# A fused diffusion-layer kernel whose instruction order comes from a planner in the kernel file: 46 shifts of places in the planner's list, and a bound on the row loads of the late modulation

## The chip, the cores and the metric

One core of one Trainium2 chip. The metric is the device time of one execution in microseconds (us); for the kernel before it is the median of 3 runs. TensorE (PE in the profile) multiplies matrices, VectorE (DVE) and ScalarE (ACT) work on rows of 128 partitions, GpSimd (POOL) clears some memory and issues a few DMAs, SyncE (SP) issues all other DMAs. Each engine takes its own instructions in the order in which they stand in the program, and waits at the first one whose operands aren't there.

## The reference

One layer for 512 latent tokens x and 256 context tokens, model width 1024, all in float32:

```python
mod = silu(c) @ w_ada + b_ada                  # six vectors of 1024: sh1 sc1 gt1 sh2 sc2 gt2
h  = rms_norm(x, g_norm1)*(1 + sc1) + sh1      # and hc from the context likewise
aq, ak, av, dq, dk, dv, dz, da, db, ga, gd = split_cols(h @ w_in)
y_attn = window_ctx_attention(q_a, k_a, v_a, k_ac, v_ac, attn_sink)
o_dl   = bidir_delta(*dn_inputs(dq, dk, dv, da, db), s_cf, s_cb)   # gated delta rule, chunks of 64
y = sigmoid(ga)*(y_attn @ w_br_attn) + sigmoid(gd)*(y_d @ w_br_dn)
x_new = x + gt1 * (y @ w_out)
x_new = x_new + gt2 * (square(relu(hm @ w_mlp1)) @ w_mlp2)         # hm: normed x_new with sc2, sh2
```

The delta rule runs forward and backward over 4 context chunks and then 8 latent chunks; each chunk needs the inverse of a triangular matrix. The late modulation is the last four of the six vectors of `mod` (gt1, sh2, sc2, gt2): they aren't needed before the output product.

## The kernel before, in words

Weights and activations are split into a high and a low part, and a product is three matmuls: high by high, high by low, low by high (`mm3`, L308, its matmuls at L313 to L315; the gate tiles at L1060; `prod`, L1547, in the feed-forward part, where Strassen-like combinations of blocks are used). `wload` (L283) loads a weight tile of 128 x 1024 on SyncE's queue (L286), ScalarE casts the high part (L291), VectorE subtracts for the low part (L296). `act` (L182) is the helper of all table functions on ScalarE, `split` (L221, L222) that of high and low parts.

The stages overlap, and in order they are: the first modulation and the norms (L246 to L321); the input products; attention (`scores` L550, `outputs` L609; L565 to L655); the chunk matrices and their inversion (L806 to L895, the inverse is a row-by-row recurrence on VectorE at L884 and L885); `combine` (L897), which joins halves of the inverses by 32x32 matmuls (L905, L906, L915, L916); the recurrence `chain_step` (L1159, matmuls of 64x64 at L1176); the gate tiles and attention's branch products that fill in between (L1060, L1106); the output products; the feed-forward part.

The late modulation (`late_mod`, L1120) has 32 rows, 8 for each of the four vectors. A row is a tile of 128 x 1024 of `w_ada` (512 KB): one DMA on SyncE's queue (L1124), one multiply with the silu of c and a sum on VectorE (L1125), one column of `modT`. The rows' tiles come from the common arena of memory, so a load waits only until its place in the arena is free. The rows are asked for in three places: three and three ahead of the two `combine` of the latent chunks and the two masked products behind them (L1306, L1318), one at a time inside the recurrence (L1356), the rest at the output products (L1436, L1439) and in the feed-forward part.

The code writes 8,024 steps (instructions) in the order of its lines: 5,857 for TensorE, 1,074 for VectorE, 849 for ScalarE, 38 for GpSimd, 206 for SyncE. `arrange` (L1804) then gives each engine its final order. `needs` (L1749) lists which steps a step must follow. `listed` (L1817) is a list planner: it walks forward in planned time with a cost for each step (`Step.cost`, L1727); on each engine it takes, of the steps that are ready by plan, the one that stands earliest in the code. On TensorE it prefers a step with the same kind of tile (whole 128x128 or smaller) if that one stands at most 50 places later. It also plans the DMA queues and the fetching of TensorE's program in blocks of 256 instructions. `gangs` are the groups of small matmuls of the recurrence, which become ready together. The planned times are used for nothing else: on the chip each engine takes its list in order, and real waits decide the times.

Of the kernel before, what the change touches and what calls it, by code (L numbers as in the profile page):

```python
# [14 lines left out]
ALU = mybir.AluOpType  # L15
# [19 lines left out]
NPL = ()  # L35
WEARLY = 0
STICK = 50
LIMIT = 1e9
ND1 = 3
NGD = 5  # L40
P = 128
# [34 lines left out]
class Buf:  # L76


    def __init__(self, arena, start, n, ap):
        self.arena, self.start, self.n, self.ap = arena, start, n, ap  # L80
# [36 lines left out]
def tile_layer(ctx: ExitStack, tc: tile.TileContext, I: dict, out: bass.AP, dbg=None):  # L117
    nc = tc.nc
    V, A, G, PE = nc.vector, nc.scalar, nc.gpsimd, nc.tensor
# [47 lines left out]
    ties, gangs = [], []  # L167
    nosync = mybir.DependencyInfo(mybir.DependencyClass.NoSync, mybir.DependencyReason.DATA)

    def tie(later, name):  # L170
        tc.add_manual_dep(later, name, nosync, reason="order")
        ties.append((later.name, name))

    def act(out_, in_, func, **kw):
# [942 lines left out]

    modT = const.tile([P, 4, 8], F32, name="modT")

    def late_mod(grp):  # L1120

        for j in range(8):
            wa = alloc(1024)
            nc.sync.dma_start(out=wa.ap, in_=I["wada2"][grp, j])  # L1124
            V.scalar_tensor_tensor(wa.ap, wa.ap, 0.5, scr.ap, op0=ALU.mult, op1=ALU.mult, accum_out=modT[:, grp, j:j + 1])  # L1125
            wa.free()
            if j == 7:
                V.tensor_tensor(modT[:, grp], modT[:, grp], bada[:, 16 + 8 * grp:24 + 8 * grp], op=ALU.add)
            yield
# [619 lines left out]
def needs(steps, ties):  # L1749

    at = {s.name: k for k, s in enumerate(steps)}
    before = [set() for _ in steps]
    for later, name in ties:
        before[at[later]].add(at[name])
    users, rings = {}, {tag: [] for tag in Step.RINGS}
    for k, s in enumerate(steps):
        for t in s.tiles:
            tag = t.split("_")[0]
            if tag in rings:
                if t not in users:  # L1760
                    rings[tag].append(t)
                users.setdefault(t, []).append(k)
    for tag, ts in rings.items():
        for old, new in zip(ts, ts[Step.RINGS[tag]:]):
            before[users[new][0]].update(users[old])
        for old, new in zip(ts, ts[1:]):
            before[users[new][0]].add(users[old][0])
    places = {}
    for k, s in enumerate(steps):
        for t, place in s.tiles.items():  # L1770
            if place:
                places.setdefault(t, (place, []))[1].append(k)
    for n, (place, ks) in enumerate(list(places.values())):
        gate = len(before)
        before.append(set())
        for (lo, hi), old in list(places.values())[:n]:
            if lo < place[1] and place[0] < hi:
                before[gate].update(k for k in old if k < ks[0])
                for o in (o for o in old if o > ks[0]):
                    before[o].update(k for k in ks if k < o)  # L1780
                    for k in (k for k in ks if k > o):
                        before[k].add(o)
        for k in ks:
            before[k].add(gate)
    wrote, read = {}, {}
    for k, s in enumerate(steps):
        for c in s.reads:
            if c in wrote:
                before[k].add(wrote[c])
        for c in s.writes:  # L1790
            before[k].update(read.pop(c, ()))
            if c in wrote:
                before[k].add(wrote[c])
            wrote[c] = k
        for c in s.reads:
            read.setdefault(c, []).append(k)
        before[k].discard(k)
    return before
# [5 lines left out]
def arrange(tc, nc, ties, gangs):  # L1804

    steps = [Step(i) for i in nc.cur_bb.bb.instructions if "Boundary" not in type(i).__name__]
    before = needs(steps, ties)
    order = mybir.DependencyInfo(mybir.DependencyClass.NoSync, mybir.DependencyReason.DATA)
    last = {}
    for k in listed(steps, before, gangs):  # L1810
        s = steps[k]
        if s.eng in last:
            tc.add_manual_dep(s.ins, last[s.eng], order, reason="order")
        last[s.eng] = s.name


def listed(steps, before, gangs):  # L1817

    n = len(steps)
    at = {s.name: k for k, s in enumerate(steps)}  # L1820
    gang = {at[name]: g for g in gangs for name in g}
    wait = {id(g): len(g) for g in gangs}
    after, left, ready = [[] for _ in before], [len(b) for b in before], [0.] * len(before)
    for k, b in enumerate(before):
        for p in b:
            if k in gang and gang[k] is gang.get(p):
                left[k] -= 1
            else:
                after[p].append(k)
    engines = ("PE", "DVE", "Activation", "Pool", "SP")  # L1830
    free, links = dict.fromkeys(engines, 0.), {"SP": 3200., "Pool": 0.}
    free["SP"] = 750.
    coming, here, out = {e: [] for e in engines}, {e: [] for e in engines}, []
    flight, whole, cold = [], True, False
    words, asked = 0, {n: 0. for n in range(3)}

    def release(ks, at_):
        for k in ks:
            ready[k] = max(ready[k], at_(k))
            left[k] -= 1  # L1840
            if not left[k]:
                if k in gang:
                    g = gang[k]
                    wait[id(g)] -= 1
                    if not wait[id(g)]:
                        go = max(ready[at[x]] for x in g)
                        for x in g:
                            heapq.heappush(coming["PE"], (go, at[x]))
                elif k < n:
                    heapq.heappush(coming[steps[k].eng], (ready[k], k))  # L1850
                else:
                    release(after[k], lambda _: ready[k])

    first = [k for k, m in enumerate(left) if not m]
    for k in first:
        left[k] = 1
    release(first, lambda _: 0.)
    for _ in steps:
        t, e = min((free[e] if here[e] else max(free[e], coming[e][0][0]), e) for e in engines if here[e] or coming[e])
        while coming[e] and coming[e][0][0] <= t:  # L1860
            heapq.heappush(here[e], heapq.heappop(coming[e])[1])
        k = here[e][0]
        if e == "PE":
            same = min((x for x in here[e] if steps[x].whole == whole), default=k)
            if same <= k + STICK:
                k = same
            block = int(words / 256 - .54) + 1
            if not steps[k].whole and asked.get(block, 0) - t > LIMIT * ((block + .54) * 256 - words):
                k = min((x for x in here[e] if steps[x].whole and steps[x].dtype.endswith("32r")), default=k)
        here[e].remove(k)  # L1870
        heapq.heapify(here[e])
        s = steps[k]
        out.append(k)
        if s.dma and e == "SP":
            if len(flight) >= 8:
                t = max(t, flight[-8])
            links[e] = end = max(t + (2400 if s.bytes > 100000 else 1600), links[e]) + s.bytes / 422
            flight.append(end)
            own = 400
        elif s.dma:  # L1880
            links[e] = end = max(t + 2400, links[e]) + s.bytes / 159
            own = 900
        else:
            own, lag = s.cost()
            if e == "PE":
                one = s.dtype.endswith("32r") or s.dtype.endswith("16") or s.ins.is_transpose
                words, had = words + (2 if one else 4), words
                block = int(words / 256 + .63)
                if block > int(had / 256 + .63):
                    asked[block] = max(t + 1100, links["SP"] - 500) + 1250  # L1890
                t = max(t, asked.get(int(had / 256 - .54), 0))
                if s.whole != whole:
                    t += 92 if whole else 130
                    cold = whole = s.whole
                elif cold and whole and s.dtype.endswith("32r"):
                    t, cold = t + 100, False
            end = t + lag
        free[e] = t + own

        def seen(x):  # L1900
            if x >= n:
                return end + 40
            f = steps[x].eng
            if not s.dma and f == e:
                return free[e] if e == "PE" else end + 10
            return end + SEEN[f]

        release(after[k], seen)
    return out


def _constants():
# [108 lines left out]
```

## Time and profile before

| | us |
|---|---|
| median of 3 runs | 898.63 (896.56 to 899.63) |
| the profiled execution | 897.89 |
| its span, first to last instruction | 896.1 |
| TensorE busy | 863.9 |
| VectorE busy | 652.8 |
| ScalarE busy | 495.3 |
| mean granted TensorE clock | 0.994 |

The span is the time from the first to the last instruction of the program; the execution's own time has some 1.8 us more around it. "Busy" is the union of an engine's instruction times. Matmuls are pipelined, so a busy TensorE needn't be at its peak. In the rows of the profile, L is a line of the kernel, the arrow in "out<-in" points from an instruction's inputs to its output, and the "<-" behind an idle time names what ended it. A row that merges several instructions gives their count behind an x.

### The profile page before, as it was taken

To read this page: it belongs to the slowest core of one execution; us is meant where nothing else is said; L and a number is where in the kernel's file an instruction comes from. 1 tells how busy PE (TensorE), PEld (TensorE's weight loads), DVE (VectorE), ACT (ScalarE), POOL (GpSimd) and SP (SyncE) were. 2 spreads that over 40 slices of the span, in tenths; PEclk is the share of its full clock that TensorE was granted. 3 is DMA by queue.
4 is the path that set the end of the run, shared out by engine and by line. 5 is a ranking of instruction groups with operands and counts; after the bars stand their busy time and mean duration, and the time that the engine had idled before them with its cause. 6 is when DMAs were issued, how large, how long until landed. Compare 5 with 4: busy or idle time off the path is not lost.

```text
span 896.1 us, 18017 instructions
## 1 busy us (share of the span) xinstructions
PE 863.9 (96%) x7564; PEld 719.5 (80%) x7564; DVE 652.8 (73%) x1111; ACT 495.3 (55%) x881; POOL 26.1 (3%) x42
## 2 busy tenths in 40 slices
PE   8999999999998998899999999999999999999998
PEld 6777778877776776777777799888997899889886
DVE  5756899977768998757787778893868377638631
ACT  5559774486668795577754335561554255425520
POOL 0000010010000001100000000000000000000000
PEclk9999999999999998999999999999999999999999
DMA  9824455442111227523144653634314331333031
GB/s 353 327 98 95 95 140 114 101 89 54 36 36 35 62 94 277 196 73 98 50 153 166 205 182 118 209 121 128 108 48 136 100 131 58 116 111 103 1 117 47
DMA packets 31985, 107.13 MB, mean 120 GB/s; under 512 B 4000, under 2 KB 4512, under 8 KB 31904
## 3 DMA queue, kind: packets, MB, share of 16 engines
q1 hardware_dynamic: 29600, 97.59, 32.2%
q0 software_dynamic: 2304, 8.39, 5.8%
q8 instruction: 59, 0.97, 0.4%
q14 instruction: 22, 0.18, 0.1%
HBM read 103.87 MB, written 2.10 MB: 118 GB/s over the span
## 4 chain that ended last, share of the span: by engine, by line
PE 65%; DVE 16%; ACT 11%; DMA 5%; issue 3%; SPq 1%; ACTq 0%; DVEq 0%
PE banks L1060 12%; PE banks L1547 11%; PE banks L314 11%; PE banks L315 11%; PE banks L313 11%; ACT m L182 3%; PE banks L1176 3%; DVE m L222 2%; DVE m L885 2%; DVE m L884 1%; ACT m L221 1%; DMA m<-in_wada 1%; DMA m<-in_wm 1%; DVE st L589 1%; ACT wh L291 1%
## 5 line engine op out<-in xcount | busy, mean ns | idle before, releaser
L313 PE MATMUL banks<-m,wh 128*128 128x512 f32 (+1 forms) x568 | 213.6, 376 | 1.4 <-ACT wh L291 1.4
L314 PE MATMUL banks<-m,wh 128*128 128x512 f32 (+1 forms) x568 | 210.4, 370 | 1.1 <-DVE m L222 1.1
L315 PE MATMUL banks<-m,wl 128*128 128x512 f32 (+1 forms) x568 | 210.5, 371 | 0.8 <-DVE wl L296 0.8
L291 ACT ACTIVATE wh<-wr 128x1024 fp32r<-128x1024 f32 (+1 forms) x92 | 90.4, 984 | 128.3 <-PE banks L314 92.3
L221 ACT ACTIVATE m<-m 128x512 fp32r<-128x512 f32 (+2 forms) x118 | 81.9, 720 | 82.4 <-PE banks L1547 18.9
L1547 PE MATMUL banks<-m,m 128*128 128x256 f32 x1008 | 123.3, 284 | 3.6 <-ACT m L221 3.1
L1547 PEld LDWEIGHTS banks<-m,m 128*128 128x128 f32 x1008 | 122.0, 192 | 5.1 <-ACT m L221 3.7
L313 PEld LDWEIGHTS banks<-m,wh 128*128 128x128 f32 x568 | 107.1, 189 | 20.7 <-ACT wh L291 2.2
L315 PEld LDWEIGHTS banks<-m,wl 128*128 128x128 f32 x568 | 106.9, 188 | 20.9 <-DVE wl L296 2.1
L314 PEld LDWEIGHTS banks<-m,wh 128*128 128x128 f32 x568 | 107.1, 189 | 18.8 <-DVE m L222 1.4
L1060 PE MATMUL banks<-m,wh 128*128 128x512 f32 x320 | 106.8, 410 | 3.6 <-ACT m L182 3.1
L222 DVE TENSOR_TENSOR m<-m,m 128x512 fp32r<-128x512 f32 (+2 forms) x118 | 92.4, 805 | 22.6 <-ACT m L221 15.8
L296 DVE TENSOR_TENSOR wl<-wr,wh 128x1024 fp32r<-128x1024 f32 (+1 forms) x76 | 84.3, 1110 | 22.9 <-ACT wh L291 17.7
L1674 DVE SCALAR_TENSOR_TENSOR m<-banks,modT,m 128x512 f32<-128x512 f32 x32 | 24.0, 750 | 74.2 <-PE banks L315 74.1
L1060 PEld LDWEIGHTS banks<-m,wh 128*128 128x128 f32 x320 | 60.1, 193 | 16.7 <-ACT m L182 3.4
L1060 PE MATMUL banks<-m,wl 128*128 128x512 f32 x160 | 65.3, 409 | 0.9 <-DVE wl L296 0.9
L314 PE MATMUL banks<-m,m 128*128 128x256 f32 (+1 forms) x136 | 45.7, 342 | 0.5 <-DVE m L321 0.5
L313 PE MATMUL banks<-m,m 128*128 128x256 f32 (+1 forms) x136 | 45.0, 345 | 0.9 <-ACT m L320 0.8
L315 PE MATMUL banks<-m,m 128*128 128x256 f32 (+1 forms) x136 | 44.5, 336 | 0.2 <-DVE m L296 0.2
L1125 DVE SCALAR_TENSOR_TENSOR m<-m,m 128x1024 f32<-128x1024 f32 x32 | 38.7, 1220 | 6.6 <-DMA m<-in_wada 6.6
L1176 PEld LDWEIGHTS banks<-m,m 64*64 64x64 f32 x1600 | 26.8, 134 | 13.6 <-issue 3.8
L1060 PEld LDWEIGHTS banks<-m,wl 128*128 128x128 f32 x160 | 30.8, 192 | 8.1 <-DVE wl L296 1.3
(252 smaller groups left out, 1318.2 us busy)
## 6 DMA issues: line engine op xcount, KB each, us to landing
m<-in_wada SPq DMA_DIRECT2D x48, 512.0 KB, 5.4
wr<-in_wm SPq DMA_DIRECT2D x40, 512.0 KB, 3.6
wr<-in_win SPq DMA_DIRECT2D x39, 512.0 KB, 3.6
m<-in_wm SPq DMA_DIRECT2D x24, 512.0 KB, 3.7
wl<-in_win POOLq DMA_DIRECT2D x16, 512.0 KB, 5.6
m<-in_xT SPq DMA_DIRECT2D x8, 512.0 KB, 5.7
wr<-in_wbr SPq DMA_DIRECT2D x16, 256.0 KB, 2.6
wr<-in_wout SPq DMA_DIRECT2D x8, 512.0 KB, 3.9
```

Source lines behind the costliest of these rows:

```text
L182: r = A.activation(out_, in_, func, **kw)
L221: A.activation(r32(hi), src, AF.Copy)
L222: (eng or V).tensor_tensor(r32(lo), src, hi, op=ALU.subtract)
L291: upper[0] = A.activation(r32(hi), raw, AF.Copy)
L296: V.tensor_tensor(r32(lo), raw, hi, op=ALU.subtract)
L313: PE.matmul(acc, w[0][:, k, :], xhi, start=(start and i == 0), stop=False)
L314: PE.matmul(acc, w[0][:, k, :], xlo, start=False, stop=False)
L315: r = PE.matmul(acc, w[1][:, k, :], xhi, start=False, stop=(stop and i == n - 1))
L1060: PE.matmul(acc.ap, w[x][:, k, :], hx[k][y], start=(k == p == 0), stop=(k == KT - 1 and p == 2))
L1125: V.scalar_tensor_tensor(wa.ap, wa.ap, 0.5, scr.ap, op0=ALU.mult, op1=ALU.mult, accum_out=modT[:, grp, j:j + 1])
L1176: runs[n].append(PE.matmul(out_, w, x, start=True, stop=True).ins.name)
L1547: PE.matmul(dst, r32(self.w[w][i][:, k * P:(k + 1) * P]), xs7[x][k][j], start=(n == 0), stop=(n == 11))
```

## The change

Three things. First, row n of the late modulation may be loaded only after the sum of row n - 3: a real wait in the DMA's own queue, and also a constraint for the planner. Second, the planner is rewritten as a class `Lists` whose `run` takes a `rank` for every step in place of the step's number, and ready steps are taken by the smallest rank. The members of a gang carry the rank of the gang's first member. Third, `settled` starts from rank = number and adds 46 shifts. An entry (engine, first, end, places) adds `places` to the rank of the steps first to end - 1 of one engine (0 TensorE, 1 VectorE, 2 ScalarE; -1 means all engines). A positive shift lets other ready steps go first, a negative one lets these go first. No instruction is added, removed or changed. The constant `LIMIT` and the branch that used it go.

```diff
-LIMIT = 1e9
+NROWS = 3
...
-    def tie(later, name):
-        tc.add_manual_dep(later, name, nosync, reason="order")
+    sync = mybir.DependencyInfo(mybir.DependencyClass.Sync, mybir.DependencyReason.DATA)
+
+    def tie(later, name, how=nosync):
+        tc.add_manual_dep(later, name, how, reason="order")
         ties.append((later.name, name))
...
+    sums = []
+
     def late_mod(grp):
 
         for j in range(8):
             wa = alloc(1024)
-            nc.sync.dma_start(out=wa.ap, in_=I["wada2"][grp, j])
-            V.scalar_tensor_tensor(wa.ap, wa.ap, 0.5, scr.ap, op0=ALU.mult, op1=ALU.mult, accum_out=modT[:, grp, j:j + 1])
+            d = nc.sync.dma_start(out=wa.ap, in_=I["wada2"][grp, j])
+            if len(sums) >= NROWS:
+                tie(d.ins, sums[-NROWS], sync)
+            r = V.scalar_tensor_tensor(wa.ap, wa.ap, 0.5, scr.ap, op0=ALU.mult, op1=ALU.mult, accum_out=modT[:, grp, j:j + 1])
+            sums.append(r.ins.name)
             wa.free()
...
-    before = needs(steps, ties)
...
-    for k in listed(steps, before, gangs):
+    for k in settled(Lists(steps, needs(steps, ties), gangs)):
...
-            block = int(words / 256 - .54) + 1
-            if not steps[k].whole and asked.get(block, 0) - t > LIMIT * ((block + .54) * 256 - words):
-                k = min((x for x in here[e] if steps[x].whole and steps[x].dtype.endswith("32r")), default=k)
...
+SHIFTS = (
+    (2, 1816, 2816, 200), (2, 535, 735, 250), (1, 5382, 5442, -40), (-1, 6758, 6788, -160), (0, 176, 196, -80),
+    (0, 341, 1841, 5), (1, 3561, 3636, 250), (2, 1435, 2435, 200), (1, 5696, 6296, 80), (-1, 6202, 7202, -80),
+    (0, 4946, 5146, -15), (-1, 345, 1345, -30), (-1, 1367, 1427, 30), (0, 15, 1015, 80), (-1, 1714, 1814, 20),
+    (-1, 6311, 7311, 40), (2, 1967, 2117, 500), (-1, 2162, 2222, 200), (2, 558, 618, -200), (-1, 1973, 2373, -10),
+    (-1, 3483, 3513, 120), (1, 6392, 6452, -500), (0, 5104, 5149, 40), (1, 4337, 4347, 60), (2, 3641, 4641, 80),
+    (0, 1261, 1661, -80), (0, 6229, 6289, 80), (2, 4516, 4916, -80), (-1, 2486, 2546, -15), (0, 6206, 6606, -30),
+    (-1, 6162, 6182, -200), (0, 189, 339, 10), (-1, 210, 230, 80), (-1, 550, 700, 80), (-1, 935, 1085, -80),
+    (-1, 746, 896, -10), (2, 6222, 6242, 80), (0, 5309, 5369, -200), (1, 1465, 2465, -500), (1, 2995, 3055, -500),
+    (-1, 3798, 4198, -80), (0, 2462, 2522, -80), (0, 2099, 3099, 120), (1, 2780, 2840, -80), (2, 2889, 2949, -500),
+    (-1, 3873, 3933, 30),
+)
+
+
+def settled(lists):
+
+    rank = list(range(lists.n))
+    for engine, first, end, places in SHIFTS:
+        for k in range(first, min(lists.n, end)):
+            if engine < 0 or lists.eng[k] == engine:
+                rank[k] += places
+    return lists.run(rank)[0]
```

To find where an entry acts, the steps are numbered in the order in which the code writes them, and matched with the trace line by line and engine by engine. Some of the entries, with the times at which the steps ran in the profiled execution:

| entry | steps | ran at, us |
|---|---|---|
| (2, 1435, 2435, 200) | 106 of ScalarE, most L182 and L221 | 167 to 282 |
| (2, 1816, 2816, 200) | 144 of ScalarE, most L182, L948 and L221 | 201 to 321 |
| (1, 1465, 2465, -500) | 138 of VectorE, most L222, L589 and L590 | 168 to 284 |
| (0, 2099, 3099, 120) | 655 of TensorE, most L1176, L1060 and L1106 | 234 to 346 |
| (-1, 3483, 3513, 120) | 18 of L806 and 12 of L1060 | 370 to 373 |
| (1, 3561, 3636, 250) | 4 of VectorE, L1065 and L296 | 377 to 387 |
| (2, 3641, 4641, 80) | 154 of ScalarE, most L1232 and L1248 | 348 to 450 |
| (-1, 3798, 4198, -80) | 400, most L1176 and L1060 | 378 to 423 |
| (-1, 6202, 7202, -80) | 1,000, most L1547 and L313 to L315 | 614 to 778 |

More of the change, by code (lines that the diff above doesn't have):

```diff
@@ L1814, in arrange @@
         last[s.eng] = s.name
[L1817 to L1827, printed above, removed]
-            else:
[L1829 to L1850, printed above, removed]
-                else:
[L1852 to L1866, printed above, removed]
-            block = int(words / 256 - .54) + 1
-            if not steps[k].whole and asked.get(block, 0) - t > LIMIT * ((block + .54) * 256 - words):
-                k = min((x for x in here[e] if steps[x].whole and steps[x].dtype.endswith("32r")), default=k)
[L1870 to L1909, printed above, removed]
```

107 lines of the change are left out of this document (added).

## The prediction

> **What bounds the kernel now.** I read the page first: engine shares, then the chain that ended last.
>
> ```profile
> span 896.1 us, 18017 instructions
> PE 863.9 (96%) x7564; PEld 719.5 (80%) x7564; DVE 652.8 (73%) x1111; ACT 495.3 (55%) x881; POOL 26.1 (3%) x42
> ...
> PE 65%; DVE 16%; ACT 11%; DMA 5%; issue 3%; SPq 1%; ACTq 0%; DVEq 0%
> ```
>
> TensorE (PE) is busy 96% of the span, and the change leaves every matmul in. So it can give back only what TensorE loses: time without a matmul, time at a lower clock, and what is hidden inside "busy" (turns between tile sizes), which the page doesn't show. Next I read the stages, cut where the work changes: the front, the input products, attention, the late rows, the recurrence, output products and feed-forward part, the end. After the limits of a stage come its length, then the busy us of PE, PEld, DVE, ACT and POOL, the granted clock, the DMA share and GB/s.
>
> ```profile
> 0.00:50.00 50.00, 45.00 (x328) 34.47 (x329) 31.06 (x65) 26.11 (x40) 0.95 (x5) 1.00 0.86 324
> 50.00:175.00 125.00, 123.90 (x1045) 99.79 (x1044) 104.30 (x207) 85.10 (x135) 10.39 (x12) 1.00 0.48 107
> 175.00:345.00 170.00, 163.08 (x1424) 127.61 (x1423) 141.39 (x243) 127.35 (x252) 8.49 (x13) 1.00 0.25 64
> 345.00:385.00 40.00, 34.39 (x768) 27.35 (x767) 29.30 (x50) 20.17 (x38) 5.18 (x10) 0.87 0.64 224
> 385.00:500.00 115.00, 110.26 (x1706) 85.39 (x1705) 86.70 (x170) 70.95 (x193) 1.04 (x2) 1.00 0.36 120
> 500.00:875.00 375.00, 370.00 (x2227) 330.87 (x2226) 255.81 (x375) 164.51 (x223) 0.00 (x0) 1.00 0.35 114
> 875.00:896.00 21.00, 17.31 (x77) 14.01 (x75) 4.23 (x5) 1.06 (x1) 0.00 (x0) 1.00 0.13 50
> ```
>
> Length less PE busy: 5.00, 1.10, 6.92, 5.61, 4.74, 5.00 and 3.69 us idle. The first and last are the loads of the start (DMA share 0.86) and the last sum and store; I count both as fixed. Only 345 to 385 has a clock below 1.00. There are two holes in it, each shown here with the stretch behind it:
>
> ```profile
> 349.34:352.69 3.35, 0.00 (x1) 0.00 (x0) 3.08 (x6) 0.00 (x0) 0.00 (x0) 0.79 0.97 346
> 352.69:358.00 5.31, 5.31 (x109) 4.47 (x110) 3.51 (x6) 2.35 (x4) 1.04 (x2) 0.50 0.98 355
> 375.82:378.08 2.26, 0.00 (x1) 0.00 (x1) 2.20 (x5) 2.13 (x4) 1.04 (x2) 1.00 0.87 297
> 378.08:382.00 3.92, 3.92 (x10) 3.12 (x11) 3.83 (x9) 2.64 (x6) 0.00 (x0) 0.57 0.52 157
> ```
>
> After each hole TensorE runs at about half clock. The first costs 3.35 + 5.31 x (1 - 0.50) = 6.0 us, the second 2.26 + 3.92 x (1 - 0.57) = 3.9 us. Together, 9.9 us is the largest single thing an order could win.
>
> The Trainium skill, "TensorE: Matmul & The Clock Gate", Part 1, puts the fall to half rate behind an idle window of about 3.4 us. The first hole agrees; the second, 2.26 us long, should by that rule be free of it, and its row says 0.57. By the page the second hole would be worth 2.3 us, and my sum, which takes half of it, would win 0.8 us less; the row decides.
>
> Who ended the idle time (us in all, times, longest):
>
> ```profile
> PE banks L916 <- issue: 3.4, 1, 3.4
> PE banks L1547 <- ACT m L221: 3.1, 3, 2.0
> PE banks L1106 <- ACT m L948: 1.6, 1, 1.6
> PE banks L1176 <- ACT m L1215: 1.5, 1, 1.5
> ...
> PE banks L314 <- DVE m L222: 1.1, 1, 1.1
> ...
> PE banks L623 <- DVE m L222: 1.0, 1, 1.0
> PE banks L1060 <- ACT m L182: 0.8, 1, 0.8
> ```
>
> Beyond the holes these are single waits of 1 to 2 us on ScalarE or VectorE, mostly one instruction that stood behind another in an in-order queue. An order can remove these, and open others.
>
> **The change part by part.** (1) *The wait.* Row n's load may not start before the sum of row n - 3. Why the first hole is there, from the DMA queues: the kernel's whole count of instruction packets; then 344.5 to 350.3; then 350.3 to 352.6.
>
> ```profile
> q8 instruction: 59, 0.97, 0.4%
> ```
> ```profile
> q1 hardware_dynamic: 443, 1.63, 82.4%
> ...
> wr<-in_win SPq DMA_DIRECT2D x1, 512.0 KB, 6.2
> ```
> ```profile
> q1 hardware_dynamic: 230, 0.84, 100.4%
> q8 instruction: 1, 0.02, 2.5%
> ```
>
> 59 packets for 2 x 7564 matmuls and weight loads are 256 instructions each: this is TensorE's program. None comes in the 5.8 us before 350.3, while the data queue is full; one comes after 350.3, and TensorE resumes at 352.69. I read the hole as TensorE out of instructions, its fetch held behind data. What filled the queue (SyncE's issues, VectorE's sums, ScalarE's casts):
>
> ```profile
> 336.39 0.42 SPq L1124 DMA_DIRECT2D m<-in_wada  x1
> ...
> 343.51 3.33 SPq L1124 DMA_DIRECT2D m<-in_wada  x4
> 348.25 0.33 SPq L286 DMA_DIRECT2D wr<-in_win  x1
> 351.49 0.33 SPq L1124 DMA_DIRECT2D m<-in_wada  x1
> 351.91 0.38 SPq L286 DMA_DIRECT2D wr<-in_win  x1
> 353.85 3.46 SPq L1124 DMA_DIRECT2D m<-in_wada  x3
> ...
> 451.27 2.51 SPq L1124 DMA_DIRECT2D m<-in_wada  x5
> 454.93 11.74 SPq L286 DMA_DIRECT2D wr<-in_wbr  x2
> ```
> ```profile
> 345.25 1.22 DVE L1125 SCALAR_TENSOR_TENSOR m<-m,m 128x1024 f32<-128x1024 f32 x1
> ...
> 350.23 1.23 DVE L1125 SCALAR_TENSOR_TENSOR m<-m,m 128x1024 f32<-128x1024 f32 x1 [0.27 <-DMA m<-in_wada]
> ```
> ```profile
> 360.23 1.06 ACT L291 ACTIVATE wh<-wr 128x1024 fp32r<-128x1024 f32 x1 [4.46 <-PE banks L1060]
> 375.04 1.06 ACT L291 ACTIVATE wh<-wr 128x1024 fp32r<-128x1024 f32 x1 [5.42 <-issue]
> 376.12 1.28 ACT L1339 ACTIVATE m<-m 32x512 f32<-32x512 f32 x2
> 377.43 0.60 ACT L182 ACTIVATE m<-banks 128x512 f32<-128x512 f32 x1
> ```
>
> After the single row of 336.39, the last two of the four issued from 343.51 to 346.84 need the first and second sum, done at 346.47 and 351.46: the last would start 4.6 us or more later. That takes at least one transfer of 512 KB out of the queue while the fetch waits; at 346 GB/s one is 1.5 us. Alone, then, the wait would win between nothing (the fetch stands behind the earlier rows) and the whole 6.0 us; with the order also changed, so that matmuls, rows and fetch meet otherwise, I take the whole.
>
> What the wait can cost: SyncE's queue is in order. Behind the held row stands the weight load of 348.25; it lands 6.2 us later, at 354.4, and its cast starts at 360.23. Held to 351.5, it is 3.2 us late and still has 2.6 us to spare. The five rows of 451.27 would be held in the same way, with the branch weights of 454.93 behind them. I count nothing for both; without cover each would cost up to a 3 us hole with its clock, 6 us. The wait itself occupies no computing engine.
>
> (2) *The 46 shifts.* They add no instruction; they change which of several ready instructions an engine takes first, by up to 500 places. Many span half of the program, so an edit can't be priced by itself. I bound by stage: below, a loss as large as stalls are here (see the rivals); above, all the idle time. At 375 to 378 the fault is plain: ScalarE stood idle 5.42 us ahead of a cast of L291, and the eviction L182 that TensorE needed stood behind it and two copies, until 378.03. No entry moves these ScalarE steps. Two move what stands beside them: one puts 18 half products (L806) and 12 gate matmuls of 370 to 373 back by 120 places, one puts four VectorE steps of 377 to 387 back by 250. So this hole may close (3.9 us) or stay; I take half, 2.0 us.
>
> For the single waits I take half: 6.92 / 2 = 3.5 in attention, 4.74 / 2 = 2.4 in the recurrence, 5.00 / 2 = 2.5 in the last part. Half, because ScalarE (127.35 of 170) and VectorE (141.39 of 170) have little room in attention, while they have much from 500 on (164.51 and 255.81 of 375). From 50 to 175 there is 1.1 to win; I take nothing. The front's entries stay behind its loads: nothing.
>
> Against that I set one new stall of the first hole's kind, 6.0 us, since moving thousands of steps by places, not times, will hit some queue wrongly.
>
> Sum against the profiled execution: 6.0 + 2.0 + 3.5 + 2.4 + 2.5 - 6.0 = 10.4 us off its 897.89 (its span and 1.8 us around it), 887.5. The median of the three runs, 898.63, lies 0.7 above that execution: **888.2 us** for a median after.
>
> (3) *The rest.* The removed limit of 1e9 never decided anything (its right side is far above any time), the members of a gang now carry the place of their first, and the planner's code is host work: nothing.
>
> **Rivals.** *A: the first hole stays.* The fetch waits behind the first rows and the weights, which the rule leaves in flight: 888.2 + 6.0 = 894.2. For it: three rows still may be under way, and no entry moves SyncE's steps or TensorE's from 346 to 370. Against it: the matmuls that ran before 346 are put back by up to 120 places, so that they mix with these. The Trainium skill, "Runtime: NRT & Kernel Launch", section on instruction fetch mechanics, says that blocks of 256 instructions are fetched while the current one runs, a cost mostly hidden; by that the hole would be something else and rival A the result. The packets' size agrees, the hole of 3.35 us speaks against "hidden" at this place.
>
> *B: nearly everything goes.* All idle time from 50 to 875 and the clock: 1.1 + 6.9 + 9.9 + 4.7 + 5.0 = 27.6 us, 871.0. Fewer turns between tile sizes would help. Against it: these waits are the ends of in-order queues in three engines at once.
>
> *C: nothing on balance*, 898.6: what is won is given back elsewhere.
>
> *D: slower, by stalls in attention.* A moved stretch puts an instruction whose operand isn't there ahead of one that TensorE needs, as L291 before L182 now. An entry moves 655 matmul steps that ran from 234 to 346 back by 120 places, others move ScalarE's steps of 167 to 321 by 200 and VectorE's of 168 to 284 forward by 500. Price: 6.0 us each with the half clock. With the holes at 345 to 385 unmended and 8.4 us won in the other stages, slower begins at the second such stall; three give 898.6 - 8.4 + 18.0 = 908.2.
>
> **How the numbers follow.** Forecast 0.50; A 0.16; B 0.09; C 0.07; D 0.18. The forecast's own range is 882 to 894 (no new stall, or two). The range of 8 in 10 takes in A and C, most of the forecast's low side and the near part of B and D: 874 to 902. About 0.3% (2.7 us) is what a measurement of this kernel can tell from no change. Faster by more than that: the forecast, A and B, 0.75; within: 0.07; slower: 0.18.
>
> **What would show it.** The DMA view should show row loads no longer four in a row near 345, no hole put down to "issue" there, and a clock of 1.00 in every slice. The waits of TensorE should show L182 gone from the longest and the sum of idle time from 50 to 875 near 14 us instead of 23.4. Shifts that fail show as new waits of TensorE on ScalarE or VectorE of over 2 us between 175 and 345, with a clock below 1.00 behind them. The prediction is wrong if the idle time falls and the time doesn't (turns inside "busy" grew), or if the held rows make TensorE wait for weights.

## The result and the profile after

The changed kernel took 884.72 us (median of 4 runs, 884.62 to 885.44) against 898.44 us before (896.56 to 899.63): a ratio of 0.9851, 95% interval 0.9833 to 0.9869, 13.7 us faster. The forecast was 888.2 us, 10.4 us faster than its base of 898.63.

The page of the changed kernel, engine shares and chain:

```profile
span 882.9 us, 18024 instructions
PE 858.9 (97%) x7564; PEld 717.2 (81%) x7564; DVE 652.3 (74%) x1111; ACT 496.9 (56%) x881; POOL 26.0 (3%) x42
...
PE 74%; ACT 10%; DVE 7%; DMA 5%; issue 2%; SPq 0%; DVEq 0%; ACTq 0%
```

The work is the same: 7,564 matmuls, and VectorE and ScalarE as busy as before (the 7 instructions more are all semaphore instructions). TensorE's idle time fell from 32.2 to 24.0 us (span less busy), and its busy time by 5.0 us. Those two make the 13.2 us by which the span is shorter. Busy time can fall with equal work because it holds stretches at half clock: by the rows of the holes, here and in the prediction, these cost 2.66 + 1.69 us before and 1.7 us now, 2.6 of the 5.0 us. The other 2.4 us aren't traced.

The same stages, cut at the same times (length, then busy us of PE, PEld, DVE, ACT, POOL, clock, DMA share, GB/s). Work after a gain lies earlier than before, so a row holds slightly later work than the row of before. The last row cuts attention's stage off at the first hole of now:

```profile
0.00:50.00 50.00, 44.91 (x328) 34.26 (x328) 30.82 (x64) 25.64 (x40) 0.95 (x5) 1.00 0.87 325
50.00:175.00 125.00, 124.89 (x1053) 101.67 (x1052) 106.24 (x211) 85.59 (x135) 10.39 (x12) 1.00 0.47 104
175.00:345.00 170.00, 163.13 (x1540) 126.48 (x1540) 141.36 (x241) 127.46 (x253) 8.47 (x13) 1.00 0.28 69
345.00:385.00 40.00, 36.85 (x810) 29.39 (x810) 31.70 (x56) 24.41 (x43) 5.72 (x12) 0.97 0.69 222
385.00:500.00 115.00, 113.15 (x1584) 89.17 (x1583) 87.51 (x169) 71.70 (x192) 0.51 (x1) 1.00 0.40 129
500.00:875.00 375.00, 371.92 (x2241) 333.25 (x2240) 253.89 (x373) 162.10 (x220) 0.00 (x0) 1.00 0.35 112
```
```profile
175.00:341.48 166.48, 161.40 (x1521) 125.05 (x1521) 137.84 (x239) 125.14 (x247) 7.51 (x12) 1.00 0.27 66
```

Idle time of TensorE from 50 to 875 is now 0.1, 6.9, 3.2, 1.9 and 3.1 us, 15.1 in all; it was 23.4. The 6.9 of attention's row can't be set against the 6.92 of before: the first hole, 1.79 us, lies in this row now and lay in the row from 345 before. Without it attention has 166.48 - 161.40 = 5.1 us. Who ended the idle time (us, times, longest), a row of before that the prediction's list leaves out, then the changed kernel:

```profile
PE banks L1060 <- ACT m L182: 3.1, 2, 2.3
```
```profile
PE banks L1062 <- ACT m L184: 3.0, 2, 2.5
PE banks L908 <- issue: 1.8, 1, 1.8
...
PE banks L1554 <- ACT m L223: 1.5, 1, 1.5
```

L184 and L1062 are L182 and L1060 of before, L1554 and L223 are L1547 and L221, L908 and L918 are L906 and L916. So there are still two holes. The second is the same wait as before. The first is again put down to "issue", at 32x32 matmuls, but at an earlier run of them: L908 and not L918, ahead of which this execution lists no idle time. Each hole with a stretch behind it:

```profile
341.48:343.27 1.79, 0.00 (x0) 0.00 (x0) 1.79 (x2) 0.97 (x2) 0.95 (x2) 1.00 0.63 160
344.30:347.71 3.41, 3.41 (x9) 2.65 (x8) 2.16 (x4) 2.15 (x6) 0.00 (x0) 0.50 0.92 290
370.60:373.13 2.53, 0.00 (x1) 0.00 (x0) 2.45 (x6) 2.39 (x4) 1.04 (x2) 1.00 0.75 230
373.13:380.00 6.87, 6.87 (x147) 5.62 (x150) 6.20 (x12) 4.90 (x11) 0.00 (x0) 1.00 0.14 53
```

The first hole cost 3.35 us and 2.66 us of clock; it now costs 1.79 and 3.41 x 0.50 = 1.7 us. The second is a little longer (2.26 us before), without a slower clock behind it in this execution. Another execution of the changed kernel (`after_again`, below) has the same hole with a slow stretch behind it:

```profile
370.27:372.81 2.54, 0.01 (x1) 0.01 (x1) 2.46 (x6) 2.41 (x4) 1.04 (x2) 1.00 0.73 231
374.27:377.69 3.42, 3.42 (x9) 2.67 (x8) 3.38 (x8) 2.74 (x7) 0.00 (x0) 0.50 0.02 7
```

So the 1.7 us of the second hole's clock are won in the one execution and not in the other. With them some 3.9 of the 9.9 us went, where the forecast counted 8.0.

What surrounds the first hole now: the DMA queues from 338.5 to 341.4, just ahead of it, and the next row loads on SyncE's queue.

```profile
q1 hardware_dynamic: 110, 0.37, 33.8%
q8 instruction: 1, 0.02, 2.8%
```
```profile
343.66 3.20 SPq L1128 DMA_DIRECT2D m<-in_wada  x3
```

Three rows in a row, the counterpart of the four that the prediction blamed, start only behind this hole, and ahead of it the data queue is a third busy. So they can't be its cause. Still, the whole came out better than forecast. The experiments say where from.

### The profile page after: what moved, and what is told of

The parts are those of the page before. It is cut to its first block, busy times and chain, and to the rows that moved or that the text cites. A ratio compares the mean times of both kernels' runs of the same rounds, so it can differ in the third digit from the quotient of the medians.

```text
span 882.9 us, 18024 instructions
## 1 busy us (share of the span) xinstructions
PE 858.9 (97%) x7564; PEld 717.2 (81%) x7564; DVE 652.3 (74%) x1111; ACT 496.9 (56%) x881; POOL 26.0 (3%) x42
## 4 chain that ended last, share of the span: by engine, by line
PE 74%; ACT 10%; DVE 7%; DMA 5%; issue 2%; SPq 0%; DVEq 0%; ACTq 0%
PE banks L315 14%; PE banks L316 14%; PE banks L317 14%; PE banks L1554 13%; PE banks L1062 7%; DMA m<-in_wada 4%; PE banks L1183 2%; ACT m L184 2%; ACT m L950 1%; PE banks L635 1%; ACT wh L293 1%; ACT m L223 1%; PE banks L1108 1%; DMA wr<-in_win 1%; DVE m L224 1%
## 5 line engine op out<-in xcount | busy, mean ns | idle before, releaser
L315 PE MATMUL banks<-m,wh 128*128 128x512 f32 (+1 forms) x568 | 213.5, 377 | 0.0
L1554 PE MATMUL banks<-m,m 128*128 128x256 f32 x1008 | 125.7, 283 | 1.6 <-ACT m L223 1.5
L1554 PEld LDWEIGHTS banks<-m,m 128*128 128x128 f32 x1008 | 123.3, 191 | 2.5 <-ACT m L223 2.0
L315 PEld LDWEIGHTS banks<-m,wh 128*128 128x128 f32 x568 | 107.1, 189 | 18.9 <-issue 1.2
L223 ACT ACTIVATE m<-m 128x512 fp32r<-128x512 f32 (+2 forms) x118 | 81.9, 720 | 71.3 <-PE banks L1554 14.7
L1062 PE MATMUL banks<-m,wh 128*128 128x512 f32 x320 | 106.9, 408 | 3.5 <-ACT m L184 3.0
L1062 PEld LDWEIGHTS banks<-m,wh 128*128 128x128 f32 x320 | 59.3, 190 | 16.6 <-ACT m L184 3.3
L1062 PE MATMUL banks<-m,wl 128*128 128x512 f32 x160 | 64.7, 404 | 0.0
L316 PE MATMUL banks<-m,m 128*128 128x512 f32 (+1 forms) x136 | 45.9, 341 | 0.5 <-DVE m L323 0.5
L315 PE MATMUL banks<-m,m 128*128 128x256 f32 (+1 forms) x136 | 45.1, 343 | 0.9 <-ACT m L322 0.8
L317 PE MATMUL banks<-m,m 128*128 128x256 f32 (+1 forms) x136 | 45.0, 336 | 0.0
L1062 PEld LDWEIGHTS banks<-m,wl 128*128 128x128 f32 x160 | 30.6, 191 | 6.3 <-issue 0.2
```

The lines of the kernel that those rows point to most:

```text
L223: A.activation(r32(hi), src, AF.Copy)
L315: PE.matmul(acc, w[0][:, k, :], xhi, start=(start and i == 0), stop=False)
L316: PE.matmul(acc, w[0][:, k, :], xlo, start=False, stop=False)
L317: r = PE.matmul(acc, w[1][:, k, :], xhi, start=False, stop=(stop and i == n - 1))
L1062: PE.matmul(acc.ap, w[x][:, k, :], hx[k][y], start=(k == p == 0), stop=(k == KT - 1 and p == 2))
L1554: PE.matmul(dst, r32(self.w[w][i][:, k * P:(k + 1) * P]), xs7[x][k][j], start=(n == 0), stop=(n == 11))
```

## The experiments

The theory formed on the two profiles was that the shifts carry the gain, mostly from 385 on, and that the rule on the rows is worth little. The rival was the forecast's: the rule is worth most of the first hole's 6.0 us. Ratios are to the kernel before, on the same chip, with 95% intervals; medians of before were 898.7 to 899.9 us in these comparisons.

**The rule alone** (`rule_only`):

```diff
-SHIFTS = (... 46 entries ...)
+SHIFTS = ()
```

> The rule of three rows, as a wait and as a constraint of the planner, without any of the 46 shifts. Theory (the shifts carry the gain, by closing single waits from 385 on): 895 to 898, that is 0.5 to 3.5 us below before. Rival (the bound on the rows carries it, as the prediction's first term had it): 890 or less, with no idle time of TensorE put down to issue near 345 and a clock of 1.00 there.

898.53 us, ratio 0.9992 (0.9974 to 1.001): no gain is measured, and the median lies 0.5 us above the theory's range, so the rule is worth less than either side had it. The hole of the rule alone, its stretch behind it, and its row loads on SyncE's queue:

```profile
349.89:353.70 3.81, 0.00 (x1) 0.00 (x1) 3.81 (x6) 0.00 (x0) 0.00 (x0) 0.80 1.01 370
353.70:359.00 5.30, 5.30 (x109) 4.46 (x110) 2.36 (x5) 2.35 (x4) 1.03 (x2) 0.50 0.80 279
```
```profile
345.98 1.45 SPq L1128 DMA_DIRECT2D m<-in_wada  x3
348.78 0.33 SPq L288 DMA_DIRECT2D wr<-in_win  x1
351.66 1.47 SPq L1128 DMA_DIRECT2D m<-in_wada  x2
```

Three rows and a weight tile in flight go with a DMA share of 1.01 in the hole, and the hole is 3.81 us, longer than before. The row that was the last of four, at 346.5, is now loaded at 351.7, and nothing is won by it.

**The shifts alone** (`shifts_only`):

```diff
-NROWS = 3
+NROWS = 99
```

> All 46 shifts, no rule on the rows. Theory (the shifts carry the gain): 884 to 888, at most 3 us above the changed kernel. Rival (the bound on the rows carries it): 890 or more, with a hole of 3 us or more near 345.

885.17 us, ratio 0.9838 (0.9815 to 0.9861): the whole gain. Four rows in a row are back, and the longest hole for instructions, 1.7 us, is as long as the changed kernel's:

```profile
343.66 3.15 SPq L1128 DMA_DIRECT2D m<-in_wada  x4
```

The rival falls.

**The wait taken out, the order kept** (`rule_plan`):

```diff
-                tie(d.ins, sums[-NROWS], sync)
+                tie(d.ins, sums[-NROWS])
```

> The changed kernel's order on every engine, with the real wait of the row loads taken out: the planner still counts with it. Theory (the wait itself is worth little): within 1.5 us of the changed kernel, 883 to 886.5. Rival (the wait keeps the fetch of TensorE's program free): rows start earlier, the hole near 341 grows from 1.8 us to 3 us or more, and the time is 888 or more.

882.71 us, ratio 0.9812 (0.9788 to 0.9837). The changed kernel itself, run again on another chip, gave 0.9828 (below), its first measurement 0.9851; the intervals overlap, so no effect of the wait itself is measured, and no gain of it. (The median lies 0.3 us below the theory's range.) The row loads without the wait:

```profile
345.71 2.45 SPq L1128 DMA_DIRECT2D m<-in_wada  x3
...
352.09 8.38 SPq L1128 DMA_DIRECT2D m<-in_wada  x5
```

With the wait they were three from 343.66 and five from 352.52 in 8.40 us. So with this order the rows lie about as far apart without the wait as with it; the rival's earlier rows didn't come.

**Rows of a quarter of the size, in the order of before** (`quarter_rows`):

```diff
-            nc.sync.dma_start(out=wa.ap, in_=I["wada2"][grp, j])
-            V.scalar_tensor_tensor(wa.ap, wa.ap, 0.5, scr.ap, op0=ALU.mult, op1=ALU.mult, accum_out=modT[:, grp, j:j + 1])
+            nc.sync.dma_start(out=wa[:, :256], in_=I["wada2"][grp, j][:, :256])
+            three = lambda ap: ap[:, 256:].rearrange("p (n c) -> p n c", n=3)
+            part = wa[:, :256].unsqueeze(1).broadcast_to([P, 3, 256])
+            V.scalar_tensor_tensor(three(wa.ap), part, 0.5, three(scr.ap), op0=ALU.mult, op1=ALU.mult, accum_out=modT[:, grp, j:j + 1])
```

(The planner was given the full sizes, so that every engine's order is that of before. Three quarters of each row's data and products are left out, and a sum on VectorE takes 0.95 us in place of 1.22.)

> The kernel before, with the same order on every engine, but each row of the late modulation loads only its first 256 of 1024 columns (128 KB in place of 512 KB), and its sum runs over those 256 columns three times, 768 in all: three quarters of the late modulation's products are left out. Theory (the hole at 349 is the fetch of TensorE's program held behind row loads): the hole of 3.35 us and the half clock behind it are gone, 891 to 893.5. Rival (the hole has another cause): it stays at 3 us or more, and the time is within 1.5 us of before, 897 to 900.

894.76 us, ratio 0.9959 (0.9943 to 0.9975). Between the two: the first hole and what follows it in this run:

```profile
350.48:352.13 1.65, 0.00 (x1) 0.01 (x1) 1.65 (x4) 0.00 (x0) 0.00 (x0) 1.00 0.69 258
352.13:358.00 5.87, 5.87 (x114) 4.83 (x115) 3.20 (x8) 2.35 (x4) 1.04 (x2) 0.71 0.63 190
```

Three quarters less row data halves the hole (3.35 to 1.65 us) and shortens the slow stretch: 5.87 x (1 - 0.71) = 1.7 us against 2.66. So the rows' data is part of the cause, as far as the shorter sums, which change with it, aren't; and a hole of about 1.7 us stays with a quarter of the data. The changed kernel's hole, 1.79 us, has that size, with a data queue a third busy ahead of it.

**The shifts in the order of their stages** (`first_13`, `first_26`, `first_35`, then all). A list planner that runs forward changes little ahead of the steps that an entry names, so the groups can be added one after the other. All have the rule.

```diff
-SHIFTS = (... 46 entries ...)
+SHIFTS = (... the entries with first < 1400; < 3100; < 5200 ...)
```

> The rule of three rows and the 13 shifts whose first step is below 1400 (the front, the input products, the chunk matrices). Theory (the gain grows stage by stage, as the lead of the changed kernel's matmuls over before does): 896 to 898, 1 to 3 us below before. Rival (the forecast's view that this stage holds nothing to win): within 1 us of the rule alone, 897.5 to 899.5.

> The rule and the 26 shifts whose first step is below 3100: attention's 13 are added. Theory: 894 to 896, some 2 us more than the 13, since the lead grew by 1.7 us from 175 to 345. Rival (half of attention's idle time goes, as forecast): 3.5 us more than the 13. Rival on the other side (moved stretches open stalls in attention): slower than the 13.

> The rule and the 35 shifts whose first step is below 5200: the 9 of the late rows and the recurrence are added. Theory: 887 to 889, the largest step of all, 5 to 8 us, since the lead grew most between 345 and 500. Rival (the holes near 350 were mended by attention's shifts already, by moving matmuls past the rows): 2.5 us more at most, 892 or more.

> The changed kernel itself, on the same chip as its parts: 884 to 886, with the last 11 shifts worth some 3 us over the first 35.

| kernel | median us | ratio, 95% interval | step, us |
|---|---|---|---|
| rule, no shift | 898.53 | 0.9992 (0.9974 to 1.001) | |
| first 13 (front) | 896.14 | 0.9972 (0.9955 to 0.9989) | -2.4 |
| first 26 (and attention) | 896.56 | 0.9987 (0.9969 to 1.0004) | +0.4 |
| first 35 (and recurrence) | 888.86 | 0.9893 (0.9866 to 0.9919) | -7.7 |
| all 46 (and last part) | 882.55 | 0.9828 (0.9801 to 0.9854) | -6.3 |

(The first row is from another chip.) The front gives some 2 us, at the edge of what the intervals tell apart; attention's 13 bring the median no further; the recurrence's 9 give most, the last 11 nearly as much. The rows of the first 13 and the first 35 came out as the theory had them; attention's 2 us did not come, and the last 11 gave twice the 3 us.

That attention's 13 bring nothing in the end doesn't mean that they change nothing. The stages with the first 26, where before had 163.08 of 170, 34.39 of 40 and 110.26 of 115 us busy:

```profile
175.00:345.00 170.00, 163.48 (x1543) 126.74 (x1542) 141.35 (x240) 127.40 (x253) 8.47 (x13) 1.00 0.28 69
345.00:385.00 40.00, 36.80 (x805) 29.10 (x804) 31.24 (x55) 23.45 (x42) 5.19 (x10) 0.96 0.64 213
385.00:500.00 115.00, 108.24 (x1552) 83.89 (x1551) 82.85 (x164) 69.33 (x191) 1.04 (x2) 0.99 0.36 114
```
```profile
PE banks L918 <- issue: 1.5, 1, 1.5
PE banks L908 <- issue: 1.4, 1, 1.4
```

In place of the hole of 3.35 us there are two of 1.4 and 1.5 us, and idle time from 175 to 385 is 9.7 us in place of 12.5. From 385 to 500 it is 6.8 in place of 4.7: in these executions the recurrence and the turn to the output products lose again most of what was won. With the 35 it is 1.7 there (113.31 of 115 us busy). A group's step in the table is therefore not what its own stage wins.

What the last 11 did is seen in the waits of TensorE from 505 to 875. First, with the first 35 shifts (from 510), then with all:

```profile
PE banks L1554 <- ACT m L223: 3.1, 3, 2.0
PE banks L316 <- DVE m L224: 1.0, 1, 1.0
PE banks L1465 <- DVE m L1436: 0.6, 1, 0.6
PE banks L1554 <- DVE m L224: 0.5, 2, 0.3
```
```profile
PE banks L1554 <- ACT m L223: 1.5, 1, 1.5
PE banks L316 <- DVE m L323: 0.3, 1, 0.3
```

Waits of 5.2 us are down to 1.8: 3.4 us of the 4.5 between these two executions (888.41 and 883.90 us). The rest, and that the medians lie 6.3 apart, isn't traced.

**Which of the recurrence's nine** (`first_26_and_3`, `first_26_and_6`):

```diff
 SHIFTS = (... the 26, and of the nine ...
+    (0, 4946, 5146, -15), (0, 5104, 5149, 40), (2, 4516, 4916, -80),          # first_26_and_3
+    (1, 3561, 3636, 250), (-1, 3483, 3513, 120), (1, 4337, 4347, 60),         # first_26_and_6
+    (2, 3641, 4641, 80), (-1, 3798, 4198, -80), (-1, 3873, 3933, 30),
```

> The rule, the 26 shifts below 1400 and 3100, and of the next 9 only the three whose first step is above 4400: TensorE's 4946 to 5145 by -15 and 5104 to 5148 by 40, ScalarE's 4516 to 4915 by -80. Theory (the step from 26 to 35 shifts is won at the turn from the recurrence to the output products, where these three act): 888 to 890, like the 35. Rival (it needs the recurrence's own six shifts): 893 or more.

> The rule, the first 26 shifts, and of the next 9 only the six of the recurrence, whose first step is below 4400; the three of the run before are left out. Theory (these six put the recurrence ahead of the gate products and so leave more of them for the turn to the output products): 888 to 891, like the 35, with more than 80 gate matmuls behind the last one of the recurrence in place of 73. Rival (only all nine together close the waits): 893 or more.

The three: 898.65 us, ratio 0.9992 (0.9976 to 1.0009). The six: 889.51 us, ratio 0.9883 (0.9862 to 0.9903). The first theory, that the three at the turn do it, fell; the six do it all but alone. What they change at the turn is the number of gate matmuls left behind the last matmul of the recurrence. With the 26 shifts (behind 450.8), and with the six added (behind 445.7):

```profile
L1062 PE MATMUL banks<-m,wh x48: 387/389/486, 451.2 to 470.1; 128*128 128x512 f32 x48
L1062 PE MATMUL banks<-m,wl x25: 389/389/497, 450.9 to 470.3; 128*128 128x512 f32 x25
```
```profile
L1062 PE MATMUL banks<-m,wh x55: 389/389/500, 445.7 to 467.5; 128*128 128x512 f32 x55
L1062 PE MATMUL banks<-m,wl x28: 388/389/395, 446.1 to 467.7; 128*128 128x512 f32 x28
```

73 gate matmuls against 83 (48 + 25, 55 + 28; with the three it is 73, as with the 26): the recurrence ends 5 us earlier since its own matmuls stand ahead of gate products, and the gate products then cover the stretch in which the recurrence's result is normed, transposed and split, and the branch weights come in. The stages of the 26, then of the 26 and six:

```profile
385.00:445.00 60.00, 57.12 (x1240) 43.69 (x1239) 41.44 (x98) 43.32 (x143) 1.04 (x2) 0.97 0.26 81
445.00:510.00 65.00, 61.12 (x358) 48.49 (x357) 50.17 (x78) 30.21 (x55) 0.00 (x0) 1.00 0.53 172
```
```profile
385.00:445.00 60.00, 58.37 (x1299) 44.42 (x1301) 44.40 (x104) 45.14 (x148) 0.52 (x1) 1.00 0.24 76
445.00:510.00 65.00, 63.92 (x339) 52.23 (x332) 49.80 (x78) 29.36 (x49) 0.00 (x0) 1.00 0.52 178
```

Idle time from 445 to 510 falls from 3.9 to 1.1 us, from 385 to 445 from 2.9 to 1.6, and the clock there goes from 0.97 to 1.00, which is 57.12 x 0.03 = 1.7 us. That is 5.8 of the 6.2 us between these two executions (897.31 and 891.08; the medians are 7.1 apart). The 1.7 us are a single slow stretch, which another execution needn't have. That the cover by gate matmuls closes the waits at the turn is argued from these rows; the count of matmuls and the idle time are shown.

**The last 20 without the first 26** (`last_20`, the rule kept):

```diff
-SHIFTS = (... 46 entries ...)
+SHIFTS = (... the 20 entries with first > 3100 ...)
```

> The rule and the last 20 shifts only; the first 26 (front and attention) are left out. Theory (the 26 won 2 us, and what they won near 350 was given back by 500): 883 to 886, at most 2.5 us above the changed kernel. Rival (the later shifts were fitted to what the earlier ones leave, and do little without them): 890 or more.

889.52 us, ratio 0.9883 (0.9862 to 0.9904): between the two, 0.5 us short of the rival. The later shifts win 1.2% alone. In this run's waits the second hole is the largest:

```profile
PE banks L1062 <- ACT m L184: 5.4, 2, 4.6
PE banks L918 <- issue: 2.7, 1, 2.7
```

The 26 that give little by themselves are worth some 5 us ahead of the 20 (0.9883 against 0.9828): the groups don't add up. The stages above suggest how: what the 26 win up to 385 is mostly lost at the recurrence without the nine, and kept with them.

**The eviction ahead of the cast** (`evict_first`), an attempt at a version that beats both:

```diff
+    for late in (3537, 3545, 3566):
+        before[late].add(3563)
     return before
```

> The changed kernel, in which ScalarE does the eviction that TensorE waits for at 370 (step 3563, helper L184) ahead of the cast and the two copies that stand before it now; nothing else moves but two clears on GpSimd. Theory (the second hole is the place of the eviction in ScalarE's queue): the hole of 2.5 us shrinks below 0.8 us, the time falls by 2 to 4 us against the changed kernel. Rival (the next operand is late anyway): the wait takes another name and the time is within 1 us of the changed kernel.

882.55 us, ratio 0.9808 (0.9787 to 0.9828). ScalarE now does the eviction as soon as the product is done:

```profile
371.00 0.60 ACT L184 ACTIVATE m<-banks 128x512 f32<-128x512 f32 x1 [5.71 <-PE banks L1062]
371.62 1.28 ACT L1346 ACTIVATE m<-m 32x512 f32<-32x512 f32 x2
372.93 1.06 ACT L293 ACTIVATE wh<-wr 128x1024 fp32r<-128x1024 f32 x1
```

TensorE's waits in the whole execution, and its stretch around the place where the second hole was:

```profile
PE banks L918 <- issue: 2.9, 1, 2.9
...
PE banks L1062 <- ACT m L184: 1.1, 1, 1.1
```
```profile
369.00:375.00 6.00, 5.94 (x56) 4.64 (x55) 5.79 (x13) 3.88 (x6) 1.04 (x2) 1.00 0.46 152
```

TensorE is idle for 0.06 us from 369 to 375: the hole of 2.5 us is gone, as the theory of the queue had it. (The 1.1 us are a wait for another eviction, at 379.3.) The time doesn't show it. Against the changed kernel's 0.9828 (0.9801 to 0.9854) the intervals overlap, and in this execution a hole for instructions of 2.9 us stands at L918, where the changed kernel had none. So the cause of the second hole is shown; as a faster version it is inconclusive.

## Why the prediction was right, and where its steps were wrong

The time lay in the range: 10.4 us forecast, 13.7 us measured. That was in good part luck, for the terms were off in both directions and cancelled.

- *The first hole, 6.0 us by the wait with the order.* The step that failed is "I take the whole" for the rule. The rule alone won nothing (0.9992) and left a hole of 3.81 us. The shifts, without the rule, took the whole gain. In the changed kernel 1.79 + 1.7 us of the hole's price remain, so 2.5 of the 6.0 us went, and by order. Rival A ("the first hole stays") had the better view of the wait: three rows under way are enough. The reading of the hole itself, instructions held behind data, holds in part: quarter rows halved it, but some 1.7 us stand behind a queue a third busy too. (Ahead of the hole of before the queue was at 82.4% by the prediction's own row, busy and not full.)
- *The second hole, 2.0 us.* Right that no entry moves the eviction ahead of the cast: it stayed, 2.53 us, and `evict_first` shows that this place in the queue is its cause. Half of it didn't go. Only its half clock was absent, and in the second profiled execution it was there.
- *Attention, 3.5 us.* Half as large: idle time fell from 6.9 to 5.1 us, 1.8 us. By itself it brought the time nothing: in the execution of the 26 the recurrence lost most of it again.
- *The recurrence and the turn, 2.4 us.* Idle time from 385 to 500 fell by 2.9 us (4.74 to 1.85), near the forecast. But the step of the 35 is 7.7 us: without the nine the earlier gains are mostly lost here, which the forecast, stage by stage, didn't see.
- *The last part, 2.5 us.* Right in its place: idle time fell by 1.9 us (5.00 to 3.08) in the first profile and by 3.4 us in the pair of kernels above; the step of the last 11 is 6.3 us.
- *The front, nothing.* It gave about 2 us by the first 13 shifts (0.9972); 1.0 us is idle time from 50 to 175, 0.1 us where it was 1.1.
- *One new stall, 6.0 us.* None in the changed kernel. Among the subsets there is one: with the 26 and the three, TensorE waits 3.0 us up to 379 for VectorE ahead of the half products (L808), and that kernel gains nothing. So rival D's mechanism is real, in a part of the change, and at 379 rather than in attention.
- *The bound.* Faster by 27.6 us, rival B, would have needed attention and both holes.

In sum, by the two profiled executions: 16.4 us of gains were forecast and 2.5 + 1.4 + 1.8 + 2.9 + 1.9 + 1.0 = 11.5 us came, 0.8 us less with small losses elsewhere (0.6 from 345 to 385, 0.2 at both ends). The stall of 6.0 us didn't come. The remaining 2.5 of the 13.2 us (the 2.4 of above, but for rounding) lie inside TensorE's busy time, for which the forecast's sum has no term, and are not traced.

Among the signs that the prediction named, the four rows in a row are gone (three from 343.66), but `shifts_only` has them again at the same time, so they were no sign of the gain. Idle time from 50 to 875 is 15.1 us where it said near 14. The hole put down to "issue" and the clock below 1.00 are still there.

## What to carry to other kernels

A stage's idle time isn't the bound of what a new order can win there. A gain in one stage can be lost in the next (with the 26, idle time from 175 to 385 is down by 2.8 us, from 385 to 500 up by 2.0), so read where it goes before an edit is called useless. Fillers that are used up early may leave the next stage bare, so count what is left to cover a turn (73 or 84 matmuls here), not only the gaps. When stages are compared at fixed times, look which stage a hole falls in. Before a wait is given credit for removing a stall, take it out with the order kept: here the wait won nothing and the order everything. Edits of an order don't add up; to price groups of them, add them in the order of time.

## What the runs showed of the hardware

TensorE's half clock doesn't follow from a hole's length alone: a hole of 2.26 us had a stretch at 0.57 behind it, one of 2.53 us had 1.00, one of 1.65 us had 0.71. The same wait of the same kernel had 1.00 behind it in one execution (2.53 us) and 0.50 for 3.4 us in another (2.54 us). A single execution's price for a hole is uncertain by that, 1.7 us.

TensorE stands still for instructions at runs of small matmuls, and not only when the DMA queues are full: 1.65 to 1.8 us at DMA shares of 0.63 to 0.69 in the hole (quarter rows; the changed kernel, with 0.34 for data just ahead of it), 3.35 to 3.8 us at 0.97 to 1.01. The share alone doesn't set the length: `evict_first` left TensorE's order as it was and got a hole of 2.86 us at L918, at 0.63. That the engine outruns the fetching of its program is shown by where the holes begin. Counted in TensorE's matmuls, weight loads and semaphore instructions, all 18 holes over 1 us that the 14 traces put down to "issue" begin behind number 5,825, 6,081 or 6,593; these lie 256 and 512 apart, one packet and two. Each of them stands at 32x32 matmuls, and each trace has one or two of the three. Quarter rows apart, no run changed what makes a packet late. The Trainium skill, "Runtime: NRT & Kernel Launch", section on instruction fetch mechanics, calls the cost of this fetch mostly hidden; over the whole kernel that is so (59 packets before, and one hole), at the runs of 32x32 matmuls it isn't.
